# Weight sums of the FFN units: from VectorE, in one instruction, to GpSimd, in four pieces

## The chip, the cores and the metric

The kernel runs on one core of a Trainium2 chip. The metric is the device time of one execution in microseconds. The engines are TensorE (PE in the profile; PEld is its weight load), VectorE (DVE), ScalarE (ACT), GpSimd (POOL) and SyncE (SP, which only issues transfers).

## The reference

Two layers of a decoder trunk on 512 positions behind 16 learned ones (T = 528 columns), model width 1024. Each layer has a normed input projection, eight heads of forgetting attention, four of retention, an output projection, and a SwiGLU FFN of width 2816, which is the part of interest:

```python
    hn = rmsnorm(h, ffn_norm_g)
    ff = jax.nn.silu(jnp.einsum('bld,df->blf', hn, w_gate)) * jnp.einsum('bld,df->blf', hn, w_up)
    return h + jnp.einsum('blf,fd->bld', ff, w_down)
```

Everything is float32. The kernel gets that from the matrix engine by splitting each operand into a high part (a cast to the engine's format) and a low part (the rest), and adding three products: high by high, high by low, low by high.

## The kernel before

The activations lie transposed: eight tiles of 128 model rows by T columns. A tile f of 128 FFN rows (22 in all) needs two blocks of weights, gate and up, each 128 x 1024 (eight slices of 128 columns, the second four being rows 512 to 1023 of the model). Tiles 0 to 2 are computed plainly. Tiles 3 to 21, class `Unit`, compute gate and up together by a Strassen-like scheme: the columns of x are split in two halves, the model rows in two halves, and seven products in place of eight serve all. These products need sums and differences of the weights' halves, and of x's (`x_forms`).

A unit's weights come in three tiles. `a`, a raw tile, is the gate weights; `b`, a fraw tile, the up weights, to whose first half a GpSimd transfer adds the gate's first half while it lands; and `s`, an Sw tile, takes in its second half (slices 4 to 7) up's second half plus up's first half, the second again by an adding transfer of GpSimd (L908). raw has three buffers, shared with the plain tiles' weights and with w_down, fraw and Sw two.

From them come four sets of weights, each split by a cast on ScalarE into whi or fwhi and a subtraction on VectorE into wlo or fwlo (`splits`, L869 and L870): w1 is a; w2 is -s, after s's first half was set to its second half plus a's first half (L917; the negated cast is L918, the low part L919); w3 is b; w4 is a's second half, after s's first half was added to it (L928). So a sum for w4 comes behind that for w2, and a's tile and s's tile are free for the next load only behind w4's sum.

TensorE runs in an order written out by hand: the plan is a list of steps, and only TensorE's instructions keep it. For the other engines a scheduler orders instructions by when it reckons them ready; every queue then runs in order, so an instruction that waits holds all behind it. SP issues the plain loads, and its next one waits as well when a tile is not yet free.

In a unit, TensorE adds w1, w2 and w3 products into one bank x (psa), and between them ScalarE copies the bank's state into a tile e: `keep`, L947, three copies per unit. The next product into x has to wait for the copy. w4 and others go into a two-bank tile (psd). L881 is the matrix product of all units, L1016 that of w_down, L217 that of the plain tiles. Units 3 to 6 form a first round after the plain tiles, and they carry the w_down products of tiles 0 to 2; further rounds have four, four, four and three units.

Of the kernel before, what the change touches and what calls it, by code (L numbers as in the profile page):

```python
# [16 lines left out]
NK = D // 128  # L17
# [3 lines left out]
DEPTH = 2  # L21
# [7 lines left out]
HB = NK // 2  # L29
# [10 lines left out]
def hybrid_kernel(ctx, tc, x_t, w_in, w_fl, w_out, w_gate, w_up, w_down, vecs, b_fg, rope, decay, mask, ident, out_t):  # L40
    nc = tc.nc
# [13 lines left out]
    vec = const.tile([128, vecs.shape[1]], F32, name="vec")  # L55
# [214 lines left out]
    def at(tag, dt=F32R, shape=(128, T), bufs=None):  # L270
        return phase["att"].tile(list(shape), dt, name=tag, tag=tag, bufs=bufs)

    def fft(tag, dt=F32R, shape=(128, T), bufs=None):
        return phase["ffn"].tile(list(shape), dt, name=tag, tag=tag, bufs=bufs)
# [79 lines left out]
    V_ATTN, V_FFN, V_FIN, V_GN = 0, 2 * NK, 4 * NK, 5 * NK  # L354
# [439 lines left out]
    def ffn(l, st, real, last):  # L794
# [73 lines left out]
        def splits(hi, lo, src):  # L868
            nc.scalar.copy(hi, src)  # L869
            nc.vector.tensor_sub(lo, src, hi.bitcast(F32))  # L870
# [17 lines left out]
        class Unit:  # L888
# [12 lines left out]
            def load(self):  # L901
                if "a" not in self.t:
                    for n, src, pool, tag, bufs in (("a", w_gate, wp, "raw", 3), ("b", w_up, phase["ffn"], "fraw", 2)):
                        self.t[n] = pool.tile([128, NK, 128], F32, name=tag, tag=tag, bufs=bufs)
                        nc.sync.dma_start(self.t[n], src[l, self.f])
                    s = self.t["s"] = fft("Sw", F32, (128, NK, 128), 2)
                    nc.sync.dma_start(s[:, HB:NK], w_up[l, self.f][:, HB:NK])
                    nc.gpsimd.dma_start(s[:, HB:NK], w_up[l, self.f][:, 0:HB], accum_op=ALU.add)  # L908
                    nc.gpsimd.dma_start(self.t["b"][:, 0:HB], w_gate[l, self.f][:, 0:HB], accum_op=ALU.add)  # L909

            def make1(self, hi, lo):
                splits(hi, lo, self.t["a"])


            def make2(self, hi, lo):
                a, s = self.t["a"], self.t["s"]
                nc.vector.tensor_add(s[:, 0:HB], s[:, HB:NK], a[:, 0:HB])  # L917
                nc.scalar.activation(hi, s, AF.Copy, scale=-1.0)  # L918
                nc.vector.scalar_tensor_tensor(lo, s, -1.0, hi.bitcast(F32), ALU.mult, ALU.subtract)  # L919

# [3 lines left out]


            def make4(self, hi, lo):
                a, s = self.t["a"], self.t["s"]
                nc.vector.tensor_add(a[:, HB:NK], a[:, HB:NK], s[:, 0:HB])  # L928
                splits(hi, lo, a[:, HB:NK])

            def bank(self, n):
                def go():
# [53 lines left out]
        def down_job(p, f0, f1):  # L986

            n = f1 - f0
            t = {}

            def load():
                if t:
                    return
                t["r"] = wp.tile([128, NK, 128], F32, name="raw", tag="raw", bufs=3)
                for s in range(2):
                    nc.sync.dma_start(t["r"][:, s * n:s * n + n], w_down[l, 2 * p + s, :, f0:f1])

            return add_job(load=load, make=lambda hi, lo: splits(hi, lo, t["r"][:, 0:2 * n]), n=2 * n)
# [223 lines left out]
        return steps  # L1222

    neg = const.tile([128, DEPTH * HB], F32, name="neg")
    for i in range(DEPTH):
        nc.vector.tensor_scalar_mul(neg[:, HB * i:HB * i + HB], vec[:, V_FFN + NK * i + HB:V_FFN + NK * i + NK], -1.0)
    gf = const.tile([128, NK], F32, name="gf")
    nc.vector.tensor_scalar_mul(gf, vec[:, V_FIN:V_FIN + NK], RSC)

    def layer(l):  # L1230
# [5 lines left out]
        ret = [{} for _ in range(RH)]  # L1236

        def ropes():
            for i, n in enumerate(("cr", "sr")):
                t = at(n, F32)  # L1240
                nc.sync.dma_start(t, rope[i])
                nc.vector.scalar_tensor_tensor(t, t, RSC, ly["R"], ALU.mult, ALU.mult)
                ly[n] = t
# [66 lines left out]
        for g in range(2):  # L1310
# [15 lines left out]
                      ret_places(3, 52, 45.5, 47.5, 57.5, 55.5, 58.5, 60, 64.1, 63, 64.2))  # L1326
        plan += [op[3], op[7], op[11], op[15]] + op[16:]
        up = ffn(l, ff, real, real)
        plan += [lambda: enter("ffn"), start_ffn] + up
        return plan  # L1330
# [78 lines left out]
```

## Time and profile before

Three runs gave 1272.17 to 1274.06 us.

| what | value |
|---|---|
| median of the runs | 1273.28 us |
| the profiled execution: time, span | 1271.45 us, 1269.6 us |
| TensorE busy | 1254.7 us, 99% |
| VectorE busy | 952.7 us, 75% |
| ScalarE busy | 687.7 us, 54% |
| GpSimd busy | 330.2 us, 26% |
| mean granted TensorE clock | 0.998 |
| first cast of an Sw tile, layer 0 and layer 1 | 316.94 and 941.63 us from the span's start |

Times of rows are microseconds from the span's start, then the duration. A row of waits reads: engine, output, line, what it waited for, then us in total, times, longest. In a timeline row, the bracket at the end is the engine's idle time just before it and what ended that. A row of the chain of waits names work of one engine that followed itself without a gap. A group row gives count, busy us and mean ns of one, then the idle time before them.

### The profile page before, as it was taken

How to read it: one execution, taken by the hardware profiler on the slowest of the kernel's cores; microseconds unless marked ns; L12 is line 12 of the kernel's file. 1: busy time of each engine (PE TensorE's matmuls, PEld its weight loads, DVE VectorE, ACT ScalarE, POOL GpSimd, SP SyncE). 2: the span in 40 equal slices, each digit the busy share in tenths (PEclk: the TensorE clock that was granted, in tenths of full speed). 3: DMA queues.
4: the chain of work that ended last, by engine and by line, in shares of the span. 5: the costliest groups of instructions: out<-in, count | busy, mean ns of one | idle time of the engine just before them, and what ended most of it. 6: DMA issues, size and time to landing. Idle time of an engine off the chain costs nothing.

```text
span 1269.6 us, 23847 instructions
## 1 busy us (share of the span) xinstructions
PE 1254.7 (99%) x9271; PEld 1196.5 (94%) x9271; DVE 952.7 (75%) x1769; ACT 687.7 (54%) x1246; POOL 330.2 (26%) x598
## 2 busy tenths in 40 slices
PE   9999999999999999999999999999999999999997
PEld 8999999999999999999999989998789999999996
DVE  8877756779777777777786877467897777777766
ACT  7666545676444444444456665557764444444444
POOL 3355546421111111110025545554201111111100
PEclk9999999999999999999999999999999999999999
DMA  6322222226555555553323232222456655555521
GB/s 218 93 75 84 87 85 77 66 68 165 155 147 150 150 150 150 150 150 108 101 77 118 67 99 78 84 84 67 128 140 164 158 150 150 151 156 151 148 77 67
DMA packets 62098, 150.48 MB, mean 119 GB/s; under 512 B 7184, under 2 KB 14096, under 8 KB 61984
## 3 DMA queue, kind: packets, MB, share of 16 engines
q1 hardware_dynamic: 50576, 128.70, 30.5%
q0 software_dynamic: 10944, 19.93, 10.5%
q8 instruction: 73, 1.20, 0.4%
q10 hardware_dynamic: 464, 0.32, 0.1%
q14 instruction: 41, 0.34, 0.1%
HBM read 146.79 MB, written 2.13 MB: 117 GB/s over the span
## 4 chain that ended last, share of the span: by engine, by line
PE 93%; DVE 3%; ACT 2%; DMA 1%; issue 1%; DVEq 0%; ACTq 0%; SPq 0%
PE psd L217 29%; PE psa L881 19%; PE psd L1016 14%; PE psd L881 13%; PE psa L217 5%; PE psa L1016 4%; PE psa L418 2%; PE psa L573 2%; PE psa L507 2%; PE psa L730 1%; PE psa L700 1%; DVE ss L340 0%; DMA h<-x_t 0%; ACT whi L191 0%; PE psa L290 0%
## 5 line engine op out<-in xcount | busy, mean ns | idle before, releaser
L194 POOL TENSOR_TENSOR wlo<-raw,whi 128x128 fp32r<-128x128 f32 x504 | 259.0, 548 | 287.9 <-ACT whi L191 287.8
L217 PE MATMUL psd<-xh,whi 128*128 128x264 f32 (+1 forms) x792 | 195.8, 315 | 0.5 <-ACT whi L191 0.5
L217 PE MATMUL psd<-xl,whi 128*128 128x264 f32 (+1 forms) x792 | 186.1, 302 | 0.5 <-DVE xl L320 0.4
L217 PE MATMUL psd<-xh,wlo 128*128 128x264 f32 (+1 forms) x792 | 186.5, 303 | 0.0
L217 PEld LDWEIGHTS psd<-xh,whi 128*128 128x128 f32 x792 | 128.3, 189 | 5.5 <-ACT whi L191 1.2
L217 PEld LDWEIGHTS psd<-xh,wlo 128*128 128x128 f32 x792 | 126.8, 188 | 6.3 <-DVE wlo L194 0.4
L217 PEld LDWEIGHTS psd<-xl,whi 128*128 128x128 f32 x792 | 127.5, 189 | 5.0 <-DVE xl L320 1.2
L191 ACT CAST whi<-raw 128x512 fp32r<-128x512 f32 (+1 forms) x168 | 98.3, 613 | 49.7 <-PE psd L217 37.4
L908 POOL DMA_DIRECT2D Sw<-w_up x38 | 33.7, 888 | 324.7 <-DVE h L1023 248.7
L870 DVE TENSOR_TENSOR fwlo<-raw,fwhi 128x1024 fp32r<-128x1024 f32 (+2 forms) x62 | 64.0, 1032 | 36.3 <-ACT fwhi L869 36.1
L909 POOL DMA_DIRECT2D fraw<-w_gate x38 | 33.2, 874 | 220.2 <-DMA fraw<-w_up 145.4
L870 DVE TENSOR_TENSOR wlo<-raw,whi 128x1024 fp32r<-128x1024 f32 (+2 forms) x62 | 62.9, 1015 | 35.0 <-ACT whi L869 34.8
L869 ACT CAST whi<-raw 128x1024 fp32r<-128x1024 f32 (+2 forms) x62 | 54.9, 885 | 50.3 <-PE psd L881 38.6
L869 ACT CAST fwhi<-raw 128x1024 fp32r<-128x1024 f32 (+2 forms) x62 | 55.6, 897 | 47.2 <-PE psd L881 39.6
L881 PE MATMUL psa<-th,whi 128*128 128x264 f32 (+1 forms) x232 | 65.4, 282 | 0.0
L881 PE MATMUL psa<-th,wlo 128*128 128x264 f32 (+1 forms) x232 | 65.4, 282 | 0.0
L881 PE MATMUL psa<-tl,whi 128*128 128x264 f32 (+1 forms) x232 | 65.3, 282 | 0.0
L881 PE MATMUL psa<-th,fwhi 128*128 128x264 f32 (+1 forms) x224 | 63.4, 283 | 0.0
L881 PE MATMUL psa<-tl,fwhi 128*128 128x264 f32 (+1 forms) x224 | 63.3, 283 | 0.0
L881 PE MATMUL psa<-th,fwlo 128*128 128x264 f32 (+1 forms) x224 | 63.2, 282 | 0.0
L527 ACT ACTIVATE probs<-probs,nmax 128x144 f32<-128x144 f32 (+1 forms) x64 | 36.9, 576 | 44.2 <-DVE nmax L514 31.3
L947 ACT COPY e<-psa 128x264 f32<-128x264 f32 (+1 forms) x114 | 42.8, 375 | 28.0 <-PE psa L881 23.9
(341 smaller groups left out, 3980.1 us busy)
## 6 DMA issues: line engine op xcount, KB each, us to landing
raw<-w_in SPq DMA_DIRECT2D x54, 512.0 KB, 3.5
raw<-w_gate SPq DMA_DIRECT2D x44, 512.0 KB, 4.1
fraw<-w_up SPq DMA_DIRECT2D x38, 512.0 KB, 4.8
raw<-w_down SPq DMA_DIRECT2D x64, 256.0 KB, 2.9
Sw<-w_up SPq DMA_DIRECT2D x38, 256.0 KB, 2.6
fraw<-w_gate POOLq DMA_DIRECT2D x38, 256.0 KB, 4.1
Sw<-w_up POOLq DMA_DIRECT2D x38, 256.0 KB, 4.6
raw<-w_out SPq DMA_DIRECT2D x16, 512.0 KB, 3.5
```

The source lines that it names most:

```text
L191: pin(nc.scalar.copy(hi, job["raw"][:, c0:c1]), pinned)
L194: pin(sub(lo[:, i:i + step], job["raw"][:, c0 + i:c0 + i + step], hi[:, i:i + step].bitcast(F32)), pinned)
L217: nc.tensor.matmul(ps[1][b][:, 0:c1 - c0], w[:, wk, :], x[:, c0:c1], start=(k == 0 and i == 0), stop=(k == n - 1 and i == 2))
L418: nc.tensor.transpose(ps[:, 128 * j:128 * j + 128], src[:, o:o + 128], idt)
L527: nc.scalar.activation(pr, pr, AF.Exp, bias=nmax[0:nq], scale=-1.0, accum_out=rsum)
L869: nc.scalar.copy(hi, src)
L870: nc.vector.tensor_sub(lo, src, hi.bitcast(F32))
L881: nc.tensor.matmul(bank()[:, 0:b.shape[-1]], a[:, o + k, :], b, start=(fresh and k == 0 and i == 0), stop=(k == n - 1 and i == 2), skip_gr ...
L908: nc.gpsimd.dma_start(s[:, HB:NK], w_up[l, self.f][:, 0:HB], accum_op=ALU.add)
L909: nc.gpsimd.dma_start(self.t["b"][:, 0:HB], w_gate[l, self.f][:, 0:HB], accum_op=ALU.add)
L947: nc.scalar.copy(self.t["e"][:, i], self.t["x"][:, 0:w])
L1016: nc.tensor.matmul(v[:, 0:c1 - c0], a[:, s * n + k, :], b[:, c0:c1], start=(k == 0 and i == 0), stop=(k == n - 1 and i == 2))
```

## The change

Both sums are taken from VectorE. The one for w2 is made on GpSimd in `Unit.load`, right behind the two adding transfers, in four adds of one slice (128 x 128); the one for w4 is made on GpSimd in `make2`, ahead of the negated cast, in four such adds. `make4` only splits. The constant `neg` is now computed in each layer's `ropes`, for that layer alone, and not once for both in front of the layers.

```diff
@@ class Unit, load
                     nc.gpsimd.dma_start(s[:, HB:NK], w_up[l, self.f][:, 0:HB], accum_op=ALU.add)
                     nc.gpsimd.dma_start(self.t["b"][:, 0:HB], w_gate[l, self.f][:, 0:HB], accum_op=ALU.add)
+                    for i in range(HB):
+                        nc.gpsimd.tensor_add(s[:, i], s[:, HB + i], self.t["a"][:, i])
@@ make2
                 a, s = self.t["a"], self.t["s"]
-                nc.vector.tensor_add(s[:, 0:HB], s[:, HB:NK], a[:, 0:HB])
+                for i in range(HB):
+                    nc.gpsimd.tensor_add(a[:, HB + i], a[:, HB + i], s[:, i])
                 nc.scalar.activation(hi, s, AF.Copy, scale=-1.0)
@@ make4
-                a, s = self.t["a"], self.t["s"]
-                nc.vector.tensor_add(a[:, HB:NK], a[:, HB:NK], s[:, 0:HB])
-                splits(hi, lo, a[:, HB:NK])
+                splits(hi, lo, self.t["a"][:, HB:NK])
@@ in front of the layers
-    for i in range(DEPTH):
-        nc.vector.tensor_scalar_mul(neg[:, HB * i:HB * i + HB], vec[:, V_FFN + NK * i + HB:V_FFN + NK * i + NK], -1.0)
@@ layer, ropes
         def ropes():
+            nc.vector.tensor_scalar_mul(neg[:, HB * l:HB * l + HB], vec[:, V_FFN + NK * l + HB:V_FFN + NK * l + NK], -1.0)
```

In the changed kernel the first sum is L911, the second L920, the negated cast L921, its low part L922, the copy of a bank L948, the loads of w_down L997. TensorE's instructions stand in the same order. VectorE has lost the 76 sums and is otherwise the same in the FFN but for places near its start. GpSimd's row, ScalarE's and SP's differ at the start of each FFN. Three places follow, all at the start of layer 1's.

ScalarE, from the halves of the last plain tile (L191) and its result (ah) to the first unit's weights. L142 with th is the cast of x's forms, L407 with sg the silu of a plain tile, fwhi<-raw 128x768 the cast of the first w_down weights. Before:

```order
L191 CAST whi<-raw 128x512
L142 CAST ah_11899<-tq 128x512
L142 CAST th_11872<-S 128x1024
L407 ACTIVATE sg<-sg 128x512
L191 CAST whi<-raw 128x512 x2
L142 CAST ah_11991<-tq 128x512
L142 CAST th_11872<-S 128x1024
L869 CAST whi<-raw 128x1024
L918 ACTIVATE fwhi<-Sw 128x1024
L869 CAST fwhi<-raw 128x768
L407 ACTIVATE sg<-sg 128x512
```

And in the changed kernel:

```order
L191 CAST whi<-raw 128x512
L921 ACTIVATE fwhi<-Sw 128x1024
L142 CAST ah_12013<-tq 128x512
L407 ACTIVATE sg<-sg 128x512
L142 CAST th_11986<-S 128x1024
L191 CAST whi<-raw 128x512 x2
L869 CAST fwhi<-raw 128x768
L142 CAST ah_12105<-tq 128x512
L869 CAST whi<-raw 128x1024
L142 CAST th_11986<-S 128x1024
L407 ACTIVATE sg<-sg 128x512
```

The first cast of an Sw tile stood behind two ah casts, both x forms and the last plain tile's halves; now it stands ahead of them all, and it reads what GpSimd's sums write. In layer 0 it moves the same way, to behind the first ah cast. Just behind this place, on ScalarE as well, comes the cast for w4 of unit 3 (whi<-raw 128x512) between two copies of the x bank. Before:

```order
L869 CAST whi<-fraw 128x1024
L947 COPY e<-psa 128x256
L869 CAST whi<-raw 128x512
L142 CAST ah_12079<-tq 128x512
L947 COPY e<-psa 128x256
```

And in the changed kernel:

```order
L869 CAST whi<-fraw 128x1024
L948 COPY e<-psa 128x256
L142 CAST ah_12197<-tq 128x512
L869 CAST whi<-raw 128x512
L948 COPY e<-psa 128x256
```

The cast for w4 now reads GpSimd's second sum (L920) and stands right ahead of the second copy. GpSimd and SP make up the third place. GpSimd before, from the first two units on:

```order
L909 DMA fraw<-w_gate 128x512
L908 DMA Sw<-w_up 128x512
L909 DMA fraw<-w_gate 128x512
L908 DMA Sw<-w_up 128x512 x2
L909 DMA fraw<-w_gate 128x512
```

And in the changed kernel:

```order
L909 DMA fraw<-w_gate 128x512
L908 DMA Sw<-w_up 128x512
L909 DMA fraw<-w_gate 128x512
L908 DMA Sw<-w_up 128x512
L911 TENSOR_TENSOR Sw<-Sw,raw 128x128 x8
L920 TENSOR_TENSOR raw<-raw,Sw 128x128 x4
L908 DMA Sw<-w_up 128x512
L909 DMA fraw<-w_gate 128x512
L911 TENSOR_TENSOR Sw<-Sw,raw 128x128 x4
```

SP before, the loads of units 4 and 5 and the w_down weights between them, from the gate weights of unit 3:

```order
L905 DMA raw<-w_gate 128x1024
L996 DMA raw<-w_down 128x384 x2
L905 DMA raw<-w_gate 128x1024
L996 DMA raw<-w_down 128x384 x2
L907 DMA Sw<-w_up 128x512
L905 DMA fraw<-w_up 128x1024
```

And in the changed kernel:

```order
L905 DMA raw<-w_gate 128x1024
L997 DMA raw<-w_down 128x384 x2
L905 DMA raw<-w_gate 128x1024
L907 DMA Sw<-w_up 128x512
L997 DMA raw<-w_down 128x384 x2
L905 DMA fraw<-w_up 128x1024
```

GpSimd, whose FFN rows were transfers alone, now has the first sum of both units and then the second sum of unit 3 ahead of the adding transfer of unit 5. On SP, unit 5's Sw load, which overwrites the tile that unit 3's second sum reads, moved ahead of the second pair of w_down loads.

## The prediction

> **What bounds the kernel now.** First the page: busy shares, then the slices.
>
> ```profile
> PE 1254.7 (99%) x9271; PEld 1196.5 (94%) x9271; DVE 952.7 (75%) x1769; ACT 687.7 (54%) x1246; POOL 330.2 (26%) x598
> PE   9999999999999999999999999999999999999997
> ```
>
> TensorE is busy for 1254.7 of 1269.6 us. VectorE, from which the change takes work, is a quarter idle over the whole, and GpSimd, which receives it, three quarters. So a gain can come only out of what TensorE waits for. The view of TensorE's waits has nine rows, here the first and the last; the total of the nine is 6.6 us.
>
> ```profile
> PE psa L1261 <- DVE wide L61: 1.6, 1, 1.6
> ...
> PE psa L418 <- DVE psa L513: 0.2, 1, 0.2
> ```
>
> None of the nine is in a stretch that uses the weight sums: their sites are the program's start, the attention, the norm before an FFN, and the final norm (L1140). Taking 76 sums off VectorE therefore buys almost nothing; the question is whether TensorE is made to wait where it does not now. For that I looked at VectorE and GpSimd around the sums, by windows: the first units of layer 1, a unit in the middle of layer 0, the first units of layer 0, and, as the nearest thing to GpSimd working beside a full VectorE, a stretch of the attention (columns: length, then PE, PEld, DVE, ACT, POOL busy with counts).
>
> ```profile
> 940.00:951.00 11.00, 11.00 (x70) 9.89 (x69) 10.70 (x14) 6.88 (x10) 0.43 (x1) 1.00 0.47 145
> 451.00:461.00 10.00, 10.00 (x85) 10.00 (x84) 5.99 (x9) 3.54 (x4) 0.86 (x1) 1.00 0.41 116
> 316.00:327.00 11.00, 11.00 (x94) 11.00 (x93) 10.33 (x14) 6.18 (x9) 0.45 (x1) 1.00 0.37 108
> ...
> 139.18:149.83 10.65, 10.65 (x91) 10.62 (x90) 9.67 (x20) 6.33 (x13) 10.64 (x16) 1.00 0.18 51
> ```
>
> TensorE is full in all four. In the middle of an FFN VectorE has 40% of its time free (5.99 of 10). In the first units it has none (10.70 of 11, 10.33 of 11): there the last plain units still send their halves, products and x forms through it.
>
> **What is removed, and what is added.** These are the groups by shape that carry the prices, and the spread of one GpSimd piece (ns least/median/most).
>
> ```profile
> L917 DVE TENSOR_TENSOR Sw<-Sw,raw 128x512 f32<-128x512 f32 x38 | 26.1, 687 | 6.9 <-DMA raw<-w_gate 4.9 <-DMA Sw<-w_up 1.8
> L928 DVE TENSOR_TENSOR raw<-raw,Sw 128x512 f32<-128x512 f32 x38 | 25.9, 681 | 0.0
> ...
> L194 POOL TENSOR_TENSOR wlo<-raw,whi 128x128 fp32r<-128x128 f32 x504 | 259.0, 548 | 287.9 <-ACT whi L191 287.8
> ...
> L194 POOL TENSOR_TENSOR wlo<-raw,whi x504: 445/461/2073, 22.0 to 896.2; 128x128 fp32r<-128x128 f32 x168
> ```
>
> VectorE loses 26.1 + 25.9 = 52.0 us. GpSimd gets 38 units x 8 pieces = 304 pieces. The trace has no 128x128 add there, but 504 subtractions of the same shape with two SBUF inputs: 0.461 us in the median, 0.548 in the mean, 2.07 at most. At 0.548 that is 167 us of new GpSimd work, of which only what TensorE comes to wait for counts. A sum that took 0.69 us takes four pieces, 4 x 0.461 = 1.84 us undisturbed.
>
> The price of a piece depends on what VectorE does meanwhile. In the attention stretch above 16 pieces take 10.64 us, 0.665 each, beside a VectorE that is 9.67/10.65 = 91% busy: the excess over 0.461 is waiting. In the first units VectorE is 97% busy (10.70/11), with instructions of 10.70/14 = 0.76 us in the mean. A piece that finds one running waits half of it, 0.38, and takes 0.46: 0.84; one that waits for a whole one takes 1.22. I take 0.9 there, 0.7 where VectorE has some gaps, with 0.5 and 1.2 as ends.
>
> The Trainium skill bears on this in "SBUF — State Buffer", section "Who interferes with whom": a VectorE instruction with two SBUF inputs contends with a GpSimd instruction that reads SBUF, and the one that comes second blocks until the first is through. The 0.665 of the stretch agrees with a wait of that kind, and the sum by that rule alone, with the whole of an instruction waited for, would be that at 1.2 a piece, given below as the upper end.
>
> The same notes speak against the change as such: "GPSIMD Engine Reference", section "4.1 Engine selection", sends a two-input elementwise add to VectorE, as GpSimd is about twice as slow. The rows say more for this shape, 1.84 against 0.69 us, 2.7 times; by twice, a sum would cost 1.4 us and the eight pieces below 2.8 in place of 3.7 undisturbed.
>
> **In the middle of the FFN: nothing.** The unit around 450 to 466 us, period 16 us:
>
> ```profile
> 450.12 0.33 SPq L905 DMA_DIRECT2D raw<-w_gate  x1
> 454.20 0.68 DVE L928 TENSOR_TENSOR raw<-raw,Sw 128x512 f32<-128x512 f32 x1
> 454.80 0.68 DVE L917 TENSOR_TENSOR Sw<-Sw,raw 128x512 f32<-128x512 f32 x1
> 459.81 0.33 SPq L907 DMA_DIRECT2D Sw<-w_up  x1
> 464.75 0.62 ACT L869 CAST fwhi<-raw 128x512 fp32r<-128x512 f32 x1 [1.01 <-PE psd L881]
> ```
>
> The gate weights, issued at 450.12, are there by some 454.2. Four pieces for the new unit and four for the one before it take 8 x 0.5 = 4.0 us, to 458.2; even at 0.9, to 461.4. The first reader of the second sum, ScalarE's cast for the fourth product, starts at 464.75, after waiting for TensorE, and the reload of Sw leaves at 459.81 when GpSimd is through too. Slack 3.4 us at the worst price: cost 0 for 32 to 34 of the 38 units.
>
> **In layer 1's first units: the term that matters.** Rows of SP, ScalarE, VectorE, the DMA view's landing of the two gate loads (median us, the views of 927 to 935 and of 939 to 947), and the chain of waits.
>
> ```profile
> 928.62 0.33 SPq L905 DMA_DIRECT2D raw<-w_gate  x1
> 940.37 0.33 SPq L905 DMA_DIRECT2D raw<-w_gate  x1
> 946.71 0.37 SPq L907 DMA_DIRECT2D Sw<-w_up  x1
> ...
> raw<-w_gate SPq DMA_DIRECT2D x1, 512.0 KB, 3.4
> raw<-w_gate SPq DMA_DIRECT2D x1, 512.0 KB, 3.3
> ...
> 932.80 0.62 ACT L142 CAST ah<-tq 128x512 fp32r<-128x512 f32 x1 [0.37 <-DVE tq L826]
> 934.91 1.14 ACT L191 CAST whi<-raw 128x512 fp32r<-128x512 f32 x2
> 948.96 0.62 ACT L869 CAST whi<-raw 128x512 fp32r<-128x512 f32 x1 [0.98 <-DVE tq L826]
> 950.46 0.37 ACT L947 COPY e<-psa 128x256 f32<-128x256 f32 x1 [0.35 <-PE psa L881]
> ...
> 939.61 0.68 DVE L194 TENSOR_TENSOR wlo<-raw,whi 128x512 fp32r<-128x512 f32 x1
> ...
> 950.42 1.42 PE psd L881 x12
> 951.84 1.41 PE psa L881 x12
> ```
>
> Unit 3's gate weights land at 928.62 + 3.4 = 932.0. Four pieces at 0.7 end at 934.8. In the changed order ScalarE's cast of Sw (L921, 1.05 us) stands directly ahead of the ah cast that ran at 932.80, so that cast and all behind it, the halves of the last plain unit at 934.91 among them, go some 3 us later: 934.8 + 1.05 = 935.9 for 932.80. The product that reads those halves starts about 940, so TensorE does not feel it, but VectorE's last half at 939.61, which sets free the raw buffer for unit 4's gate weights, moves to about 941. That load, now at 940.37, leaves at 941.7 and lands 3.3 later at 945.0.
>
> Then GpSimd has eight pieces in a row: unit 4's first sum (it waits for this load), and only behind it unit 3's second sum (L920). 945.0 + 8 x 0.9 = 952.2. ScalarE's cast for unit 3's fourth product waits for that; it ran at 948.96. Queued behind it on ScalarE is the COPY of the x bank into e (950.46 to 950.83), and TensorE's next product into that bank starts at 951.84, once the copy is out. New end of the copy: 952.2 + 0.62 + 0.37 = 953.2, **1.4 us** after 951.84. Ends: at 0.5 a piece the sums end at 949.0, as the cast does now, cost 0; at 1.2 they end at 954.6 and the cost is 3.8. The break-even is (951.84 - 0.99 - 945.0) / 8 = 0.73 a piece.
>
> **The next unit gets it from SP.** The changed order puts unit 5's Sw load ahead of the second pair of w_down loads. The load may overwrite only when L920 has read its buffer, 952.2 in place of 946.71, and two w_down loads, the up weights and the gate weights stand behind it on SP.
>
> ```profile
> 950.57 0.86 POOL L908 DMA_DIRECT2D Sw<-w_up  x1 [29.66 <-DVE wlo L870]
> ...
> 956.81 0.69 DVE L917 TENSOR_TENSOR Sw<-Sw,raw 128x512 f32<-128x512 f32 x1 [1.77 <-DMA Sw<-w_up]
> ...
> Sw<-w_up POOLq DMA_DIRECT2D x38, 256.0 KB, 4.6
> ...
> 963.33 0.62 ACT L869 CAST fwhi<-raw 128x512 fp32r<-128x512 f32 x1 [0.98 <-PE psd L881]
> ...
> 966.18 1.43 PE psa L881 x12
> ```
>
> From SP's issue to GpSimd's accumulating load were 3.9 us (946.71 to 950.57), and from that to its landing 6.2 (VectorE's sum sat idle for it until 956.81). So the landing moves to 952.2 + 3.9 + 6.2 = 962.3 at most, or 960.7 if its median of 4.6 is taken. Eight pieces at 0.6 (VectorE is less full by then) end between 965.5 and 967.1, copies 0.99 later at 966.5 to 968.1; TensorE, itself 1.4 late, wants the bank at 966.18 + 1.4 = 967.6. Cost 0 to 0.5, at 0.9 a piece up to 2.9; I take **0.6**. The unit behind has the same shift once more, shrinking as VectorE's gaps return: 0 to 1, **0.3**.
>
> **Layer 0** has the same order with a little more room.
>
> ```profile
> 315.72 0.33 SPq L905 DMA_DIRECT2D raw<-w_gate  x1
> ...
> raw<-w_gate SPq DMA_DIRECT2D x44, 512.0 KB, 4.1
> ...
> 326.23 0.62 ACT L869 CAST whi<-raw 128x512 fp32r<-128x512 f32 x1 [0.47 <-PE psd L881]
> 327.74 0.38 ACT L947 COPY e<-psa 128x264 f32<-128x264 f32 x1 [0.89 <-PE psa L881]
> 329.15 1.45 PE psa L881 x12
> ```
>
> Its second gate load leaves at 315.72, about 1 us later in the changed order for the same reason as above, lands 4.1 after that (the page's median), at 320.8, and the eight pieces end at 328.0. The copy is out at 329.0, just before 329.15: 0, or 2.3 at 1.2 a piece. With the later Sw loads in the three units behind at 0.3 each, half the price of layer 1's, I take **1.0** (0 to 3.0).
>
> **The constant.** Its two instructions of 0.167 us stay ahead of the first use, still in the first microseconds of VectorE; nothing that TensorE waits for changes: 0, at most 0.3 either way.
>
> ```profile
> L1226 DVE TENSOR_SCALAR neg<-vec x2: 163/167/171, 3.9 to 4.0; 128x4 f32<-128x4 f32 x2
> ```
>
> **Sum.** 1.4 + 0.6 + 0.3 + 1.0 = 3.3 us of new waits of TensorE. The profiled execution took 1271.45 with a span of 1269.6, 1.8 us under the median of the runs; on the span it gives 1272.9, on the median **1276.6 us**. Ends: 0 (all hidden) and 3.8 + 2.9 + 1.0 + 3.0 = 10.7.
>
> **Rivals.** *All hidden, no change.* If VectorE gives way, so that a piece costs under 0.73 us in the first units as it does in the attention (0.665), the copy at 950.46 is in time, Sw's load leaves about when it did and the rest disappears: 0 to 2, time 1273.3 to 1275. For it: the row of 16 pieces. Against it: VectorE's instructions there are shorter (9.67/20 = 0.48 us against 0.76), so a wait for one is shorter. Within 0.2%, 2.5 us, is what a measurement here cannot tell from no change, and a weaker form of my own sum (up to 2.5) falls in it too.
>
> *Slower by twice that.* If a piece waits for a whole VectorE instruction nearly every time (1.2), the first term is 3.8 and each late Sw load pushes the next unit's gate load: 3.8 + 1.5 + 0.5 + 1.5 = 7.3, time 1280.6. For it: the maximum of 2.07 us in the spread. Against it: a median of 0.461 over all 504.
>
> *Faster.* VectorE, 52 us lighter, could shorten a wait of TensorE. The nine rows hold 6.6 us, none behind a weight sum, and the sums of the first units run beside the norm's end at most: 1 us in all, time 1272.3. To come out faster by over 2.5 us, waits of the attention would have to go, where the change moves nothing.
>
> *That the order doesn't matter,* since ScalarE's queue might run as before: no, the queue is in order and the cast stands ahead of the copy in it.
>
> **How the numbers follow.** My sum 0.45, twice of it 0.11, hidden or under 2.5 us 0.38, faster 0.06. So slower by over 0.2% 0.56, within 0.38, faster 0.06. The range reaches from the hidden case with a spread of the runs below, 1271.9, to a little above the bad case, 1281.5; the likeliest case alone is 1275.8 to 1278.5.
>
> **What would show it.** In the view of TensorE's waits after: new rows for the products at L881, released by ScalarE's copy of e (L948), one of 1 to 2 us near 952 and several of 0.2 to 0.8 in the units around 320 to 370 and 966 to 985; no such row after these. GpSimd's 128x128 adds at a mean of 0.8 to 1.0 near 945 to 953, and at 0.46 to 0.55 after 400. ScalarE idle ahead of the first cast of Sw and of the w4 cast, released by GpSimd. Wrong would be the whole if GpSimd's pieces stay near 0.5 in the first units, or if the cast starts before 950; wrong in size if waits at L881 appear in the middle units, where I say 0.

## The result

The changed kernel took 1291.08 us (median of four runs, 1286.86 to 1295.77), the kernel before 1272.72 beside it: a ratio of 1.0147, 95% interval 1.0129 to 1.0165. So it is slower by 18 us, where 3.3 were forecast. Two single executions below, one of swap (1352.99 us, at a granted clock of 0.85) and one of swap_act (4608.19 us), lie far from all others of their kernels and are in no ratio. The profiled execution of the change, the fastest of its four, took 1286.86 us with a span of 1285.1; the accounts below are of that one, 15.5 us longer in span than the profile of before.

The view of TensorE's waits has one new row, for the kind of wait that was forecast; the other nine come to 6.8 us, before 6.6:

```profile
PE psa L881 <- ACT e L948: 10.9, 9, 2.0
```

Where the time went can be read unit by unit, from when VectorE adds the two banks of a unit (L957 before, L958 after). The two rows of the first and the last unit, before and then after, from the timelines of the two kernels:

```profile
336.41 0.70 DVE L957 TENSOR_TENSOR sg<-psd,e 128x528 f32<-128x528 f32 x1
...
1232.80 0.68 DVE L957 TENSOR_TENSOR sg<-psd,e 128x512 f32<-128x512 f32 x1
```

```profile
339.33 0.70 DVE L958 TENSOR_TENSOR sg<-psd,e 128x528 f32<-128x528 f32 x1
...
1248.30 0.68 DVE L958 TENSOR_TENSOR sg<-psd,e 128x512 f32<-128x512 f32 x1
```

The difference of the two starts, us, for all that moves:

| unit | 3 | 4 | 5 | 6 | 7 | 8 | 9 to 20 | 21 |
|---|---|---|---|---|---|---|---|---|
| layer 0 | 2.92 | 4.46 | 5.59 | 6.80 | 8.44 | 8.54 | 8.2 to 8.5 | 8.21 |
| layer 1 | 9.99 | 11.96 | 15.49 | 15.67 | 16.28 | 15.70 | 15.2 to 15.8 | 15.50 |

1.6 of the first 2.92 lie ahead of the FFN (the norm's root on ScalarE starts at 298.79 where it started at 297.21); they stem from the program's start, where the second part of the first weights landed later, and other kernels below have them too or not, as the execution falls. The rest is the first round of each layer, up to unit 7: 6.6 us in layer 0, each unit adding 1.1 to 1.6, and 7.3 in layer 1, where units 3, 4 and 5 add 1.8, 2.0 and 3.5 and the next two little. From unit 8 on nothing is added.

What adds 1 us and more per unit in layer 0 is in the chain of waits of layer 0's first round:

```profile
330.83 2.64 DMA Sw<-w_up
...
334.01 7.29 DMA Sw<-w_up
341.30 0.07 issue
341.37 3.18 POOL Sw L911 x4
344.55 1.88 POOL raw L920 x4
346.43 0.02 issue
346.45 2.85 DMA Sw<-w_up
...
349.87 6.90 DMA Sw<-w_up
356.77 0.07 issue
356.84 1.90 POOL Sw L911 x3
358.74 3.33 POOL raw L920 x4
362.07 0.02 issue
362.09 2.58 DMA Sw<-w_up
```

TensorE is not in it. The chain goes round: SP's load of a unit's Sw tile, GpSimd's adding load into it, the first sum, the second sum of the unit before (queued behind the first), and that sets free the tile for the next Sw load. A turn is 346.45 - 330.83 = 15.6 us, the next 362.09 - 346.45 = 15.6. TensorE's unit in this round takes 351.08 - 336.41 = 14.7 (the rows of L957 before), so every unit is about a microsecond later than the one before it. In the later units TensorE's period is 443.69 - 427.63 = 16.1 in layer 0 and 15.5 in layer 1, and nothing is added: there the turn no longer decides.

In layer 1 the loop makes one turn only, from the Sw load at 960.89 to the next at 976.40, 15.5 us against TensorE's 14.2 a unit. After it GpSimd's row has the order turned round: unit 5's second sum (985.44) stands ahead of unit 6's first (987.12). So the 2.0 us of unit 4 there are the loop's, and the 3.5 of unit 5 are not; they come up under theory D below. In layer 0 the order is turned round once too, at 403.01, where the first round is over.

Half of a turn is the adding load. The DMA views of 313 to 395, after and then before, give the medians to landing:

```profile
raw<-w_gate SPq DMA_DIRECT2D x5, 512.0 KB, 7.3
...
Sw<-w_up POOLq DMA_DIRECT2D x4, 256.0 KB, 7.1
```

```profile
raw<-w_gate SPq DMA_DIRECT2D x6, 512.0 KB, 4.3
...
Sw<-w_up POOLq DMA_DIRECT2D x5, 256.0 KB, 5.1
```

The loads are no more than before. But SP's queue is in order, and behind the late Sw load wait w_down, the up and the gate weights; all leave together, from 330.83 to 332.72 us, where before they leave from 336.52 to 342.40:

```profile
330.83 0.33 SPq L907 DMA_DIRECT2D Sw<-w_up  x1
331.34 0.80 SPq L997 DMA_DIRECT2D raw<-w_down  x2
332.25 0.37 SPq L905 DMA_DIRECT2D fraw<-w_up  x1
332.72 0.37 SPq L905 DMA_DIRECT2D raw<-w_gate  x1
```

### The profile page after: what moved, and what is told of

The parts are those of the page before. It is cut to its first block, busy times and chain, and to the rows that moved or that the text cites. A ratio compares the mean times of both kernels' runs of the same rounds, so it can differ in the third digit from the quotient of the medians.

```text
span 1285.1 us, 24094 instructions
## 1 busy us (share of the span) xinstructions
PE 1259.3 (98%) x9271; PEld 1198.9 (93%) x9271; DVE 921.8 (72%) x1693; ACT 685.0 (53%) x1246; POOL 494.9 (39%) x902
## 3 DMA queue, kind: packets, MB, share of 16 engines
HBM read 146.79 MB, written 2.13 MB: 116 GB/s over the span
## 4 chain that ended last, share of the span: by engine, by line
PE 81%; DVE 5%; DMA 5%; POOL 3%; ACT 3%; issue 2%; ACTq 0%; DVEq 0%; POOLq 0%
PE psd L217 26%; PE psa L881 16%; PE psd L1017 13%; PE psd L881 10%; DMA Sw<-w_up 4%; PE psa L217 4%; PE psa L1017 3%; PE psa L418 2%; POOL Sw L911 2%; PE psa L573 2%; PE psa L507 2%; POOL raw L920 1%; PE psa L730 1%; PE psa L700 1%; PE psa L379 1%
## 5 line engine op out<-in xcount | busy, mean ns | idle before, releaser
L191 ACT CAST whi<-raw 128x512 fp32r<-128x512 f32 (+1 forms) x168 | 98.2, 613 | 50.5 <-PE psd L217 37.1
L911 POOL TENSOR_TENSOR Sw<-Sw,raw 128x128 f32<-128x128 f32 x152 | 86.9, 651 | 63.3 <-DMA raw<-w_gate 54.7
L920 POOL TENSOR_TENSOR raw<-raw,Sw 128x128 f32<-128x128 f32 x152 | 84.8, 623 | 22.9 <-DVE wlo L870 22.9
L870 DVE TENSOR_TENSOR fwlo<-raw,fwhi 128x1024 fp32r<-128x1024 f32 (+2 forms) x62 | 67.0, 1080 | 33.4 <-ACT fwhi L869 33.2
L1024 DVE TENSOR_TENSOR h<-psd,h 128x512 f32<-128x512 f32 (+1 forms) x69 | 47.8, 692 | 32.5 <-PE psd L1017 32.5
L881 PE MATMUL psa<-th,whi 128*128 128x264 f32 (+1 forms) x232 | 66.1, 285 | 4.9 <-ACT e L948 4.9
L881 PE MATMUL psa<-th,fwhi 128*128 128x264 f32 (+1 forms) x224 | 64.1, 286 | 6.0 <-ACT e L948 6.0
L881 PE MATMUL psa<-th,wlo 128*128 128x264 f32 (+1 forms) x232 | 65.4, 282 | 0.0
L881 PE MATMUL psa<-tl,whi 128*128 128x264 f32 (+1 forms) x232 | 65.3, 282 | 0.0
L881 PE MATMUL psa<-tl,fwhi 128*128 128x264 f32 (+1 forms) x224 | 63.3, 283 | 0.0
```

The source lines that it names most:

```text
L191: pin(nc.scalar.copy(hi, job["raw"][:, c0:c1]), pinned)
L881: nc.tensor.matmul(bank()[:, 0:b.shape[-1]], a[:, o + k, :], b, start=(fresh and k == 0 and i == 0), stop=(k == n - 1 and i == 2), skip_gr ...
L911: nc.gpsimd.tensor_add(s[:, i], s[:, HB + i], self.t["a"][:, i])
L920: nc.gpsimd.tensor_add(a[:, HB + i], a[:, HB + i], s[:, i])
L1024: nc.vector.tensor_add(sv(h[m], real), pv(ps[0], real), sv(h[m], real))
```

## The experiments

Their theories are A, the loop just described; B, the pieces on GpSimd as such, each waiting for VectorE; C, ScalarE's order, in which the first cast of Sw stands ahead of the last plain tile's work; and later D, VectorE kept waiting by GpSimd.

### Two sums in the other order (swap), ScalarE's cast put back (act_late), and both (swap_act)

```diff
+        held_sum = []
...
-                    for i in range(HB):
-                        nc.gpsimd.tensor_add(s[:, i], s[:, HB + i], self.t["a"][:, i])
+                    with tc.issue_after(held_sum[-1].ins) if held_sum else ExitStack():
+                        for i in range(HB):
+                            nc.gpsimd.tensor_add(s[:, i], s[:, HB + i], self.t["a"][:, i])
...
-                    nc.gpsimd.tensor_add(a[:, HB + i], a[:, HB + i], s[:, i])
+                    held_sum.append(nc.gpsimd.tensor_add(a[:, HB + i], a[:, HB + i], s[:, i]))
```

> The change, with one thing different: on GpSimd the second sum of a unit is queued ahead of the first sum of the next unit, where the change has it behind. Nothing else moves. Theory A (a loop: Sw load, adding load, first sum, second sum queued behind it, and only then the next Sw load; 15.5 to 16 us a turn against TensorE's 14.6 us a unit in the first round): the second sum no longer waits for the next unit's loads, the loop opens, and only the entry loss of the first unit of each layer stays: 1275 to 1280 us, TensorE's waits at L881 one per layer. Theory B (the pieces themselves, each waiting for VectorE): as many pieces beside the same VectorE, so about as slow as the change, 1287 to 1293. Theory C (ScalarE's queue, the cast of Sw drawn ahead of the last plain tile's work): that order is unchanged, so 1287 to 1293.

Measured: 1273.47 us, ratio 1.0005 (0.9996 to 1.0015). All of the loss is gone, also that of the first units, which A had left standing, and the view of TensorE's waits has no row at L881. The other engines' orders are the change's, word for word. GpSimd in the first round of layer 0, by groups for 318 to 395 us, of swap (L914 is its first sum, L923 its second) and then of the change:

```profile
L914 POOL TENSOR_TENSOR Sw<-Sw,raw 128x128 f32<-128x128 f32 x24 | 15.5, 870 | 0.0
L923 POOL TENSOR_TENSOR raw<-raw,Sw 128x128 f32<-128x128 f32 x24 | 13.7, 810 | 11.5 <-issue 11.5
```

```profile
L911 POOL TENSOR_TENSOR Sw<-Sw,raw 128x128 f32<-128x128 f32 x20 | 15.8, 809 | 16.0 <-DMA raw<-w_gate 10.3 <-DMA Sw<-w_up 5.7
L920 POOL TENSOR_TENSOR raw<-raw,Sw 128x128 f32<-128x128 f32 x20 | 14.2, 738 | 0.0
```

The pieces are as slow as in the change, 0.87 and 0.81 against 0.81 and 0.74 us: B falls as the cause of the 18 us. What differs is when the tile is free. The rows of swap:

```profile
334.53 3.09 POOL L923 TENSOR_TENSOR raw<-raw,Sw 128x128 f32<-128x128 f32 x4
337.18 4.29 POOL L914 TENSOR_TENSOR Sw<-Sw,raw 128x128 f32<-128x128 f32 x4
...
337.64 0.33 SPq L909 DMA_DIRECT2D Sw<-w_up  x1
```

The second sum is over at 337.6 and the Sw load leaves then. In the change that load left at 346.45, behind a first sum that waited until 341.37 for the adding load.

For act_late the cast is queued behind the cast of the same unit's gate weights:

```diff
-                splits(hi, lo, self.t["a"])
+                self.cast1 = splits(hi, lo, self.t["a"])
...
-                nc.scalar.activation(hi, s, AF.Copy, scale=-1.0)
+                with tc.issue_after(self.cast1.ins):
+                    nc.scalar.activation(hi, s, AF.Copy, scale=-1.0)
```

> The change, with the negated cast of Sw kept behind the cast of the same unit's gate weights on ScalarE, as it stood before the change. It matters for the first unit of each layer only. Theory A (the loop): the entry loss of some 2 to 3 us per layer goes, but the loop goes on through the first round, so 1281 to 1287 us. Theory C (ScalarE's order is the cost): everything goes, 1273 to 1275. Theory B (pieces waiting for VectorE): no change from 1287 to 1293.

Measured: 1276.73 us, 1.0039 (1.0024 to 1.0054), between what A and C said. TensorE's waits at the unit product are 3.1 us in five:

```profile
PE psa L882 <- ACT e L950: 3.1, 5, 1.1
```

The lag in layer 0 is 0.2 us at units 3 and 4, and then 1.30, 2.38 and 3.93 at units 5, 6 and 7: the loop turns as before but reaches TensorE two units later. In layer 1 it hardly begins (3.5 us at unit 3, 5.4 at unit 7); there the scheduler also put the first unit's second sum ahead of the second unit's first, so this run is not of ScalarE's order alone.

> Both: the second sum ahead of the next unit's first sum on GpSimd, and the cast of Sw behind the cast of the gate weights on ScalarE. Theory A with the entry loss from ScalarE's order: nearly all is given back, 1273 to 1276 us, with no or almost no wait of TensorE at L881. Theory B (pieces waiting for VectorE): 1285 to 1293.

Measured: 1271.56 us, 0.9995 (0.9985 to 1.0004): the kernel before, with 52 us less work on VectorE and nothing gained.

### A part of it alone: late_units, only_first, only_second, neg_only

late_units makes the sums on GpSimd for units 8 to 21 and on VectorE for units 3 to 7 (the lines of before and of the change under a condition on `self.f >= 8`).

> The sums of units 3 to 7 stay on VectorE as before the change; those of units 8 to 21 are on GpSimd as in the change, in both layers. Theory A: the later units have 16 us (15.5 in layer 1) for a turn of the loop and VectorE's gaps, so the time is that of the kernel before, 1272 to 1274 us, and TensorE has no wait at L881. Theory B (each of the 304 pieces costs something): 28 of 38 units pay, so 1280 to 1288. If the loop closes late in layer 1 all the same, where the period is 15.5 us, 1274 to 1278.

Measured: 1272.62 us, 1.0005 (0.9996 to 1.0015). 224 of the 304 pieces cost nothing.

only_first drops the second sum's lines from `make2` and restores `make4`; only_second drops the first sum's from `load` and restores VectorE's line in `make2`.

> Only the first sum (for w2) on GpSimd, the second back on VectorE in one instruction. ScalarE's cast of Sw stands early as in the change. Theory A (the loop needs the second sum queued behind the next unit's first sum): no loop, since VectorE frees the Sw tile; what is left is the entry shift from ScalarE's order: 1272 to 1277 us, TensorE's waits at L881 at most one per layer. Theory B (each piece beside VectorE costs): half the pieces, half the loss, 1280 to 1284.

> Only the second sum (for w4) on GpSimd, the first back on VectorE in one instruction. ScalarE's order is that of before. Theory A: on GpSimd nothing that waits for the next unit's adding load stands ahead of the second sum, so no loop: 1271 to 1274 us. Theory B: half the pieces, 1280 to 1284. If the second sum alone is what hurts (it frees the Sw tile later than VectorE did), 1276 to 1285 with late Sw loads in the first round.

Measured: 1271.98 us, 0.9995 (0.9986 to 1.0005), and 1272.8 us, 1.0003 (0.9994 to 1.0012). Each sum alone is free (the profile of only_second, of its slowest execution, has one wait of 0.7 us at the unit product). only_first has ScalarE's early cast and half of the pieces, so C is no cost by itself: it makes the first turn late, and what keeps the lateness is the loop, which needs both sums in one queue.

neg_only is the kernel before with the constant moved.

> The kernel before, with only the constant neg moved into the layers, as in the change. Its two instructions of 0.17 us stay in VectorE's first 12 us: no difference, 1271 to 1274 us, by every theory.

Measured: 1271.85 us, 0.9999 (0.9990 to 1.0008). The constant is worth nothing.

### A third Sw buffer (sw3)

```diff
-                    s = self.t["s"] = fft("Sw", F32, (128, NK, 128), 2)
+                    s = self.t["s"] = fft("Sw", F32, (128, NK, 128), 3)
```

> The change, with three Sw buffers in place of two. Room for the third is made by keeping the 128x128 mask of the attention in the attention's own pool and loading it once per layer; nothing else is changed, and on GpSimd the first sum of the next unit still stands ahead of the second sum. Theory A (the loop runs through the reload of the Sw tile): the reload no longer waits for the second sum just made but for the one a unit earlier, so the loop opens: 1272 to 1277 us. Theory B (the pieces beside VectorE) and theory C (ScalarE's order): unchanged, 1287 to 1293.

Measured: 1282.11 us, 1.0084 (1.0066 to 1.0101): half of the loss goes, not all. The chain of sw3 shows why. The link through the Sw tile is gone, but the first sum still stands behind the other adding load, which waits for the up weights, and these had left SP late:

```profile
330.27 6.41 DMA fraw<-w_up
...
337.24 0.86 POOL fraw L911
...
338.19 3.76 POOL Sw L913 x4
341.95 2.34 POOL raw L922 x4
```

And then it has a wait of another kind: VectorE's subtraction of the w_down weights, 0.95 us elsewhere, took 3.94. Its 3.0 us over the usual are most of a 3.7 us step in the lag between units 4 and 5 (2.31 to 6.03).

```profile
354.01 3.94 DVE L872 TENSOR_TENSOR fwlo<-raw,fwhi 128x768 fp32r<-128x768 f32 x1
```

So A, as I put it (the reload of the Sw tile), named one link of a queue in which several are tied.

### One instruction per sum (one_op)

```diff
-                    for i in range(HB):
-                        nc.gpsimd.tensor_add(s[:, i], s[:, HB + i], self.t["a"][:, i])
+                    nc.gpsimd.tensor_add(s[:, 0:HB], s[:, HB:NK], self.t["a"][:, 0:HB])
...
-                for i in range(HB):
-                    nc.gpsimd.tensor_add(a[:, HB + i], a[:, HB + i], s[:, i])
+                nc.gpsimd.tensor_add(a[:, HB:NK], a[:, HB:NK], s[:, 0:HB])
```

> The change's order, with each sum as one 128x512 instruction on GpSimd in place of four pieces of 128x128. One 128x544 product on GpSimd takes 1.37 us in the traces. Theory A: two such and one wait for VectorE each, 3 to 4.5 us for the two sums where the pieces took 5.1, bring the turn of 15.5 to 16 us down to about 14 to 15, around TensorE's 14.6 us a unit: 1273 to 1282 us. Theory B: two waits for VectorE per unit where there were eight, a quarter of the loss, 1275 to 1279; but VectorE, when it comes second, waits for a longer instruction.

Measured: 1274.74 us, 1.0022 (1.0011 to 1.0033), within what A expected and just below B's range. Groups of one_op over the whole span:

```profile
L910 POOL TENSOR_TENSOR Sw<-Sw,raw 128x512 f32<-128x512 f32 x38 | 56.7, 1493 | 63.3 <-DMA raw<-w_gate 58.2 <-DMA Sw<-w_up 5.1
L918 POOL TENSOR_TENSOR raw<-raw,Sw 128x512 f32<-128x512 f32 x38 | 56.5, 1486 | 25.0 <-DVE wlo L870 25.0
```

A sum takes 1.5 us on GpSimd in one instruction, against 4 x 0.65 = 2.6 and 4 x 0.62 = 2.5 in pieces (86.9 us for 152 pieces of L911, 84.8 for L920). Both sums together are 2.1 us shorter, and five waits of 2.3 us in all remain. But the turn is not shorter by that. The Sw loads of layer 0's first round leave so:

```profile
323.77 0.33 SPq L907 DMA_DIRECT2D Sw<-w_up  x1
...
338.96 0.33 SPq L907 DMA_DIRECT2D Sw<-w_up  x1
...
354.49 0.33 SPq L907 DMA_DIRECT2D Sw<-w_up  x1
```

The first two turns are 15.2 and 15.5 us, over TensorE's 14.7, since the adding load took 8.8 and 8.3 us to land (the DMA views of 325 to 330 and 338 to 343). What differs is the start: the first of these loads leaves 7 us earlier than in the change (330.83), so the late sums have room, and the third turn, to 368.22, is 13.7. Of the waits that remain, the chain in layer 0 runs through VectorE and not through GpSimd: its L958, 0.7 us before, takes 1.79 beside the sums.

```profile
353.24 1.79 DVE L958 SCALAR_TENSOR_TENSOR sg<-sg,R 128x528 f32<-128x528 f32 x1
```

So in the order of the change the length of the sums counts. That it counts through the turn, as A had it, is not what these rows show.

### The first sum done twice (after_twice, swap_twice), and with gaps (swap_twice_gaps)

```diff
-                    for i in range(HB):
+                    for i in list(range(HB)) * 2:
                         nc.gpsimd.tensor_add(s[:, i], s[:, HB + i], self.t["a"][:, i])
```

> The change, with the first sum's four pieces done twice over (the second time writes the same numbers again), so four more pieces per unit, in the change's order on GpSimd. Theory A: a turn of the loop grows by 1.7 us undisturbed to 3.3 us beside a full VectorE, to 17 to 19 us, which is over the 16 us of the later units too: the loop no longer dissolves after the first round, 1300 to 1350 us. If the adding load lands in 4.7 us once the first round is over, the turn is 15 and the later units still cost nothing: 1295 to 1302. Theory B with the price per piece that the change showed (18.4 us for 304 pieces, 0.06 us each): 152 more pieces, 9 us more, 1300.

> The same doubling of the first sum, but with the second sum of a unit ahead of the first sum of the next on GpSimd. Theory A: the loop is open, and the four more pieces go into GpSimd's idle time: 1272 to 1277 us. Theory B: 9 us more than the swap alone, 1282.

Measured: 1306.62 us, 1.0270 (1.0209 to 1.0330), and 1298.2 us, 1.0215 (1.0189 to 1.0242). after_twice lies where A's range begins, and B's 1300 is as near. In layer 0 its lag is 13.5 at unit 7 and at unit 21, so there the loop did dissolve after the first round; layer 1's grows from 22.8 at unit 7 to 31.2 at unit 21, where the Sw loads leave every 15.9 to 16.8 us (1124.54 to 1222.36) against TensorE's 15.5, as A would have it. swap_twice contradicts A: its loop is open, and it loses little by little, also in the late units; in layer 0 its lag grows from 3.0 at unit 3 to 10.4 at unit 21. It contradicts B's 1282 too. The rows of VectorE and GpSimd in a late unit of swap_twice (L925 is the low part of the Sw weights):

```profile
415.37 2.94 DVE L925 SCALAR_TENSOR_TENSOR fwlo<-Sw,fwhi 128x1024 fp32r<-128x1024 f32 x1 [1.94 <-ACT fwhi L924]
...
411.90 2.02 POOL L923 TENSOR_TENSOR raw<-raw,Sw 128x128 f32<-128x128 f32 x4
413.58 3.65 POOL L914 TENSOR_TENSOR Sw<-Sw,raw 128x128 f32<-128x128 f32 x8
```

VectorE's instruction, 1.22 us before the change, is issued in the midst of twelve pieces and ends at 418.31, 1.08 after the last of them (417.23). It waited for the rest of the run, not for one piece. Its successors make the silu and with it ScalarE's next copy of e late. (TensorE's waits for that copy come to 4.1 us in the view, of 19.9 us that the span is longer, so that all of the loss comes this way is argued and not shown.) Over the whole span the mean of L925 is 2.13 us; 21 of the 38 take over 1.6. In the change there are three such instructions from 300 us on, the longest in layer 1's unit 5, where the lag grows by 3.5:

```profile
985.88 3.77 DVE L870 TENSOR_TENSOR fwlo<-raw,fwhi 128x768 fp32r<-128x768 f32 x1
...
985.44 2.05 POOL L920 TENSOR_TENSOR raw<-raw,Sw 128x128 f32<-128x128 f32 x4
987.12 2.81 POOL L911 TENSOR_TENSOR Sw<-Sw,raw 128x128 f32<-128x128 f32 x4
```

That is theory D. Here VectorE ended at 989.65, ahead of the last piece (989.93). With its usual 0.95 us it began at about 988.7, behind the seventh of the eight pieces. TensorE's next wait is the longest of the nine, 2.0 us. Swap has none of these: there no such subtraction takes over 0.6 us more than usual. So swap's gain doesn't tell the loop from D in layer 1; in layer 0 the chain above does.

To give VectorE a chance between pieces, the last run has a small memset behind each.

```diff
                         for i in list(range(HB)) * 2:
                             nc.gpsimd.tensor_add(s[:, i], s[:, HB + i], self.t["a"][:, i])
+                            nc.gpsimd.memset(gap, 0.0)
...
                     held_sum.append(nc.gpsimd.tensor_add(a[:, HB + i], a[:, HB + i], s[:, i]))
+                    with tc.issue_after(held_sum[-1].ins):
+                        nc.gpsimd.memset(gap, 0.0)
```

> The kernel with the second sum first and the first sum's pieces done twice (1298 us, with 21 VectorE instructions at the low part of the Sw weights stretched from 1.2 to 2.2 to 3.6 us while GpSimd ran 12 pieces back to back), with a GpSimd memset of 128x16 behind each piece, which reads nothing. Theory D (VectorE is locked out while GpSimd's pieces follow one another without a break, and this delay reaches TensorE): VectorE gets in between two pieces, no stretched instruction is left, and most of the loss goes though GpSimd has more to do: 1274 to 1284 us. Theory B (the number and length of the pieces on GpSimd): 1298 to 1305.

Measured: 1326.76 us, 1.0442 (1.0412 to 1.0472). The remedy fails, and the rows say how:

```profile
439.15 3.29 DVE L928 SCALAR_TENSOR_TENSOR wlo<-Sw,whi 128x1024 fp32r<-128x1024 f32 x1 [1.92 <-ACT whi L927]
...
440.70 0.65 POOL L914 TENSOR_TENSOR Sw<-Sw,raw 128x128 f32<-128x128 f32 x1
441.10 0.30 POOL L915 MEMSET gap<- 128x16 f32 x1
```

The memsets don't open a gap (the next piece starts 0.06 us after a memset does), they only lengthen the run, from 0.42 to 0.47 us a piece, and VectorE still ends at 442.44, 1.04 us after the run's last row (441.40). So D's picture of VectorE kept out for the rest of a run fits this pair of runs, the longer run giving the longer wait and the greater loss; that a memset breaks the run was wrong, and the time is outside what D and B expected. A run in which the same number of pieces lies truly apart wasn't tried.

## Why the prediction was wrong, step by step

**What bounds the kernel: right.** TensorE; no wait of it could be won by relieving VectorE, and none was (swap_act and only_first, 0.9995).

**The middle of the FFN at nothing: right**, by the lag of units 8 to 21 and by late_units.

**The constant at nothing: right** (0.9999).

**The price of a piece: right, and not the cause.** I took 0.9 us in the first units; the groups give 0.81 and 0.74 in layer 0, and the eight pieces ahead of layer 1's first Sw load take 953.52 to 960.86, 0.92 each. Under nearly the same price swap loses nothing.

**The first unit of layer 1: right.** 1.4 us were forecast by the cast that waits for the second sum, ahead of the copy of e; measured 9.99 - 8.23 = 1.8 (8.23 is the lag at the norm ahead of that FFN, 929.55 against 921.32). The cast and the copy stood as forecast:

```profile
957.73 3.13 POOL L920 TENSOR_TENSOR raw<-raw,Sw 128x128 f32<-128x128 f32 x4
...
960.89 0.62 ACT L869 CAST whi<-raw 128x512 fp32r<-128x512 f32 x1 [2.79 <-POOL raw L920]
961.42 0.36 ACT L948 COPY e<-psa 128x256 f32<-128x256 f32 x1
```

**The units behind: the step that failed.** "The unit behind has the same shift once more, shrinking as VectorE's gaps return: 0 to 1, **0.3**", and for layer 0 "With the later Sw loads in the three units behind at 0.3 each, half the price of layer 1's, I take **1.0**". I had the links: the second sum behind the next unit's first sum, the Sw load behind the second sum, the adding load behind the Sw load, SP's other loads behind it. I followed them from one unit into the next and then let the effect shrink, as if lateness were a delay that slack eats up. They close into a loop, and a loop has a period: 2.6 + 0.5 + 7.3 + 3.2 + 1.9 = 15.5 us, which had to be set against TensorE's 14.7 a unit. Above it each unit adds about the difference.

Measured were 6.6 us in layer 0 for the 1.0: 1.3 at unit 3, whose next gate load left 2.8 us later (320.12 - 1.58 against 315.72) where I had put 1, and 1.1 to 1.6 at each unit behind it where I had put 0.3. In layer 1 the 0.6 of unit 4 was 2.0, in the loop's one turn there. The 0.3 of unit 5 was 3.5, and that was not the loop but VectorE kept waiting by eight pieces in a row, a term that I didn't have at all. Swap, which changes nothing but GpSimd's order, takes all of it away.

**Two sizes inside that step.** The adding load was put at 6.2 or 4.6 us to land; in layer 0 it took 7.1. With 5.1, as the load took there before, the turn would be 13.4 by my estimate and under TensorE's period. In the change SP's loads leave beside it in one bunch, and I take the loop to keep itself going by that; but one_op had 8.3 with loads that left apart (338.96 to 343.30), so the bunch is not shown to be the reason. And VectorE's own waiting was left out: I had a piece wait for VectorE, but not VectorE for a run of pieces. In the profiled execution that is 2.8 us at 985.88 (3.77 for 0.95). On this the Trainium skill, "SBUF — State Buffer", section "Who interferes with whom", had both halves: issue order decides which of the two engines blocks. I used only the half in which GpSimd is second.

**The rivals.** "All hidden" fell by the first unit already. "Slower by twice that" gave 1280.6, nearer, but for a cause that is not there, 1.2 us a piece. "Faster" fell: the nine old waits came to 6.8 us after 6.6. None of my rivals was a loop, so the range ended at 1281.5; it ended even below my own upper sum, since 10.7 us on the median would be 1284.0.

What stays open: the three runs that were not profiled took 4 to 9 us more than the one that was. The loop's turn and VectorE's waits vary with landing times, and either could make this; no run here tells which. Why an adding load takes 7 to 9 us to land in the change and in one_op, 2 us and more over the 5.1 of before, stays open too, and so does how the 7.3 us of layer 1 divide exactly between the sums' order and VectorE's waiting.

## What to carry to other kernels

When work is moved onto an in-order queue that also issues loads, write down for each buffer who frees it and what stands ahead of that on its queue, and follow it until you come back to the same load: if you do, add up the turn and compare it with the bound engine's period, because a turn that is too long costs its excess in every unit and none of it is hidden. The order of two short sums on a side engine was worth 18 us here. In the bad order their length counted as well (one instruction for four gave back 16 us); in the good one it cost nothing until a sum was doubled. And look for the smallest repair in the order first: slack that an engine shows in the mean (74% idle) doesn't tell whether a queue holds something up.

## What the runs showed of the hardware that I had not expected

A VectorE instruction that comes in the midst of GpSimd pieces issued back to back can wait for many of them: 2.94 us for a 1.22 us instruction beside 12 pieces and 3.29 beside 12 pieces with memsets between, both to the end of the run, and 3.77 for 0.95 beside 8, through seven of them. The Trainium skill's "SBUF — State Buffer" ("Who interferes with whom") says that whoever issues first holds the shared ports for the whole instruction; these rows show more than one instruction's worth, and the measurement decides. The other way round, the first sum's pieces in layer 0's first round took 0.81 us in the mean, and the longest of all 152 took 2.54 where the shortest took 0.45.

Slicing costs: a 128x512 sum with two inputs in SBUF takes 0.687 us on VectorE, 1.5 on GpSimd in one instruction (1.27 at the least), and 2.5 to 2.6 there in four pieces (1.7 in the late units, as at 526.22, where nothing stretches them), beside the same VectorE program.
